# Where a decoder kernel's weight sums leave the DMA queue: five blocks in three early stages, or forty single transfers beside a later feed-forward

## The chip, the core and the metric

One core of a Trainium2 chip runs the whole program. The metric is the device time of one execution in microseconds (us). A time without a range is the median of several runs. TensorE (PE in the profile, PEld for its weight loads), VectorE (DVE), ScalarE (ACT), GpSimd (POOL) and SyncE (SP) each work through a queue of their own. Sixteen DMA engines serve the transfers that SP and POOL issue.

## The reference, cut to what matters

The program is one inference step of a decoder with two layers, over 1024 prompt tokens and 8 sample tokens that share all weights.

- Layer 0 mixes the tokens with a gated linear recurrence and with attention into 256 memory tokens. Layer 1 mixes them with stick-breaking attention over a shared K/V and again with attention into memory.
- After each mixer comes a feed-forward block:

```python
def swiglu(h, w_gu, w_down):
    gate, up = jnp.split(h @ w_gu, 2, axis=-1)
    return (jax.nn.silu(gate) * up) @ w_down
```

The inner width is 2816, so `w_gu` is 1024 x 5632 and `w_down` is 2816 x 1024, for each layer, in float32.

## The kernel before

The tokens are split into two halves. Group 0 is 512 prompt tokens; group 1 is the other 512 and the 8 sample tokens, 520 columns in all. Every product is made of three products in a float32 form with fewer bits: each operand is split into a high part (an ACT cast, line 262 for weights) and a rest (a DVE subtraction, line 263). The weights arrive by `split_w` (line 257, on SP's queue) in tiles of 256 KB, with five raw buffers (`wraw`) and five split buffers (`wspl`).

The feed-forward (`class ffn`) runs in five parts (`PARTS`, of 5, 5, 4, 4 and 4 column blocks). A part first makes its blocks (gate, silu, up, product, split), then multiplies them into all eight rows of blocks of the accumulator `R`. As a generator it yields once a block and once every two rows. `weave` takes several such generators with a number each and draws from the one that is furthest behind its number. That order is the order of the program; a planner then orders the instructions of each engine by priority, buffers and expected times.

**The weight sums.** The last feed-forward, layer 1 of group 1 (`ffn_w`), uses a scheme with seven half-size products in place of eight, and it needs four sums of blocks of layer 1's `w_gu` for each part. `weight_sums` makes them in memory by DMAs alone: eight DMAs a part, issued by POOL, four of them plain copies (line 607) and four accumulating (`accum_op`, line 605). With five parts there are 40 DMAs of 1 MB or 1.25 MB: 10 copies out of the weights, 10 copies of one sum into another, and 20 that accumulate. Within a part most depend on the one before: a sum is copied only when it is complete.

Before a part's eight DMAs stands one mark, a POOL copy of one column (line 592). It reads a row of `R` of group 0's layer 0 feed-forward, so that it can't go before that work is there, and `tc.issue_after` keeps the part's DMAs behind it on POOL.

The order of the stages around it:

1. `a1.sample`, `a1.gate` and `f0.part(1)`, with the sums of part 0
2. `a1.merge`, `a1.mem`, `a1.mem_sample` (the sample tokens' attention into cached memory) and `f0.part(2)`, `f0.part(3)`, with the sums of parts 1 and 2
3. `f0.part(4)`, with the sums of parts 3 and 4
4. the output projection of group 1, the shared K/V of group 0, the projections of layer 1's mixer
5. `b0.sb`, `b0.mem` (layer 1's mixer on group 0) beside `f1.part(0)`, `f1.part(1)` (layer 0's feed-forward on group 1)
6. `f1.part(2)`, `f1.part(3)`, `f1.part(4)` alone

In stage 2 the sample attention (`sample_scores`, lines 911 to 919) writes its queries to memory (`qd`), reads them back broadcast to all partitions for each of the eight sample rows (line 917, SP), and multiplies them with the cache on DVE (line 918). Its cache blocks of 512 KB come over SP's queue too (line 947). POOL also issues the indirect gathers of the shared K/V pages (line 959) for the sample attention of layer 1's mixer on group 1, which comes after stage 6.

Of the kernel before, what the change touches and what calls it, by code (L numbers as in the profile page):

```python
# [1 line left out]

# [15 lines left out]
P = 128  # L18
# [4 lines left out]
def tile_decoder(  # L23
# [6 lines left out]
    nc = tc.nc  # L30
# [39 lines left out]
    def nm(s):  # L70
        uid[0] += 1
        return f"{s}_{uid[0]}"
# [23 lines left out]
    def M(dt=F32):  # L96
        return mpool.tile([P, 2, WID], dt, tag="m", name=nm("m"))
# [4 lines left out]
    def R_one():  # L102
        r = rpool.tile([P, ND, WID], F32, tag="r", name=nm("r"))
        return [r[:, k, :] for k in range(ND)]
# [14 lines left out]
    def small(shape, dt=F32, tag="sm", bufs=None):  # L119
        return spool.tile(shape, dt, tag=tag, name=nm(tag), bufs=bufs)  # L120
# [39 lines left out]
    for lv in range(7):  # L160
        m = 1 << lv
# [17 lines left out]
    def gcol(l, i, k):  # L179
        o = (l * 4 + i) * ND + k  # L180
        return par[:, o : o + 1]
# [43 lines left out]
    def drain(*gens):  # L225
        for g_ in gens:
            for _ in g_:
                pass

    def chain(*gens):  # L230
        for g_ in gens:
            yield from g_

    def weave(*streams):

        live = [[0, n, g_] for g_, n in streams]
        while live:
            cur = min(live, key=lambda e: e[0] / e[1])
            cur[0] += 1
            try:  # L240
                next(cur[2])
            except StopIteration:
                live.remove(cur)


    def pv(ps, g):
        return ps[:, 0, :G] if g == 0 else ps[:, :, : PW[1]]

    def sv(ap, g):
        return ap[:, :G] if g == 0 else ap.rearrange("p (a n) -> p a n", a=2)  # L250
# [17 lines left out]
    def proj(g, W, k0, nk, m0, xt):  # L268
        w = split_w(W, k0, nk, m0)
        ps = mmp.tile([P, 2, 512], F32, tag="mm", name=nm("mm"))  # L270
        for k in range(nk):
            wh, wl = w[k]
            for wi, (wt, xi) in enumerate(((wh, 0), (wh, 1), (wl, 0))):
                for a in range(NPC[g]):
                    o = a * PW[g]
                    nc.tensor.matmul(  # L276
                        ps[:, a, : PW[g]], wt, xt[k][:, xi, o : o + PW[g]],
                        start=(k == 0 and wi == 0), stop=(k == nk - 1 and wi == 2),
                    )
        return ps  # L280

    def split_to(dst, src):
        nc.scalar.copy(dst[0], src)  # L283
        nc.vector.tensor_sub(dst[1], src, dst[0].bitcast(F32))  # L284

    def silu(dst, ps, g):


        n = NG[g]
        x = T()  # L290
        dst = T() if dst is None else dst
        d = dst[:, :n]
        nc.vector.tensor_scalar(sv(x, g), pv(ps, g), -44.0, None, op0=ALU.max)  # L293
        nc.scalar.activation(d, x[:, :n], AF.Exp, scale=-1.0)
        nc.scalar.activation(d, d, AF.Ln, bias=1.0)
        nc.scalar.activation(d, d, AF.Exp, scale=-1.0)  # L296
        nc.vector.tensor_mul(d, d, x[:, :n])  # L297
        return dst
# [11 lines left out]
    def sq_acc(acc, src, k, n):  # L310
        if k == 0:
            nc.scalar.activation(acc[:, :n], src, AF.Square)
        else:
            t = N()
            nc.scalar.activation(t[:, :n], src, AF.Square)  # L315
            nc.vector.tensor_add(acc[:, :n], acc[:, :n], t[:, :n])  # L316
# [125 lines left out]
    def evac_raw(g, R, ps, m, acc, first, last):  # L442
        n = NG[g]
        dst = sv(R[m], g)
        if first:
            nc.scalar.copy(dst, pv(ps, g))
        else:
            nc.vector.tensor_add(dst, dst, pv(ps, g))  # L448
        if last:
            sq_acc(acc, R[m][:, :n], m, n)  # L450
# [74 lines left out]
    def gate_up_w(l, f, ops, spl, raws):  # L525

        h, n = PW[1], NG[1]
        part, o = part_of(f)
        gate, up = f * P, DFF + f * P
        src = [  # L530
# [58 lines left out]
    def weight_sums(l, parts, after):  # L589

        for i in parts:
            mark = nc.gpsimd.tensor_copy(small([P, 1], tag="mk", bufs=1), after()[:, 0:1])
            f0, nf = PARTS[i]
            w = nf * P
            s1, s2, s3, s4 = (tc.dram_tile([512, w], F32, name=nm("wsum")) for _ in range(4))
            sums.setdefault(l, {})[i] = (s1, s2, s3, s4)
            a11, a12 = (w_gu[l][r : r + 512, f0 * P : f0 * P + w] for r in (0, 512))
            a21, a22 = (w_gu[l][r : r + 512, DFF + f0 * P : DFF + f0 * P + w] for r in (0, 512))
            for d, a, add in (
                (s3, a11, False), (s1, a21, False), (s3, a21, True), (s1, a22, True),  # L600
                (s2, s3, False), (s2, a22, True), (s4, s2, False), (s4, a12, True),
            ):
                with tc.issue_after(mark.ins):
                    if add:
                        nc.gpsimd.dma_start(d, a, accum_op=ALU.add)
                    else:
                        nc.gpsimd.dma_start(d, a)
                yield

    htok = []  # L610
# [76 lines left out]
    class ffn:  # L687
# [4 lines left out]
        def part(self, pi):  # L692
            g, l = self.g, self.l
            n = NG[g]
            f0, nf = PARTS[pi]
            last = pi == len(PARTS) - 1
            mids = []
            for j in range(nf):
                pg = proj(g, w_gu[l], 0, ND, (f0 + j) * P, self.xt)
                sg = silu(None, pg, g)  # L700
                pu = proj(g, w_gu[l], 0, ND, DFF + (f0 + j) * P, self.xt)
                nc.vector.tensor_mul(sv(sg, g), sv(sg, g), pv(pu, g))  # L702
                mt = M(F32R)
                split_to((mt[:, 0, :n], mt[:, 1, :n]), sg[:, :n])
                mids.append(mt)
                yield
            if pi == 0:
                self.R = R_one()
            if last:
                self.acc = small([P, WID], tag="st", bufs=3)  # L710
            for m in range(ND):
                ps = proj(g, w_down[l], f0, nf, m * P, mids)
                evac_raw(g, self.R, ps, m, self.acc, pi == 0, last)
                if last and self.rows:
                    nc.scalar.activation(
                        self.R[m][:, :n], self.R[m][:, :n], AF.Copy, scale=gcol(l, 3, m)
                    )
                    if m == 3:
                        first_half(self)
                if m % 2:  # L720
                    yield
# [9 lines left out]
    def first_half(self):  # L731
        self.yt = [xpool.tile([P, D], F32, tag="x0", name=nm("yT")) for _ in range(CH)]
        for c in range(CH):
            ps = S()
            for k in range(4):
                nc.tensor.transpose(ps[:, k * P : (k + 1) * P], self.R[k][:, c * P : (c + 1) * P], ident)  # L736
            nc.scalar.copy(self.yt[c][:, :512], ps)
        self.ys = xpool.tile([P, D], F32, tag="x0", name=nm("yTs"))
        ps = S()
        for k in range(4):  # L740
            nc.tensor.transpose(ps[:NB, k * P : (k + 1) * P], self.R[k][:, G : G + NB], ident)
        nc.scalar.copy(self.ys[:NB, :512], ps[:NB, :])
# [647 lines left out]
    a1 = mixer_a(1, x1)  # L1390
# [5 lines left out]
    f0 = ffn(0, 0, o0.x)  # L1396
    weave((a1.core(), 22), (f0.part(0), 9))
    a1.open()
    def running():
        return f0.R[0]  # L1400

    weave((a1.sample(), 6), (a1.gate(), 4), (f0.part(1), 9), (weight_sums(1, (0,), running), 8))
    weave(
        (chain(a1.merge(), a1.mem()), 12), (a1.mem_sample(), 20), (chain(f0.part(2), f0.part(3)), 16),
        (weight_sums(1, (1, 2), running), 16),
    )
    weave((f0.part(4), 8), (weight_sums(1, (3,4), running), 16))
    xk0, xb0 = [], []
    o1 = out_proj(1, 0, M)
    drain(o1.mm(a1.xo, 0, 1))  # L1410
# [4 lines left out]
    b0 = mixer_b(0, xb0)  # L1415
    weave((b0.heads(), 8), (o1.finish(), 17))
    b0.open()
    f1 = ffn(1, 0, o1.x)
    weave((chain(b0.sb(), b0.mem()), 24), (chain(f1.part(0), f1.part(1)), 18))
    drain(f1.part(2), f1.part(3), f1.part(4))  # L1420
    xk1, xb1 = [], []
    o0 = out_proj(0, 1, M)
    drain(o0.mm(b0.xo, 0, 1))
# [7 lines left out]
    f0 = ffn(0, 1, o0.x)  # L1431
# [9 lines left out]
    f1 = ffn_w(1, o1.x, 4)  # L1441
# [34 lines left out]
```

## Time and profile before

| | |
|---|---|
| median of 3 runs | 2572.91 us (2565.16 to 2581.46) |
| profiled execution | 2567.6 us, span 2565.9 us |
| PE busy | 2513.8 us, 98% |
| PEld, DVE, ACT, POOL busy | 85%, 62%, 47%, 3% |
| DMA | 358.19 MB, mean 140 GB/s |
| queue of SP (hardware_dynamic) | 301.08 MB, 39.6% of the 16 engines' span |
| queue of POOL (software_dynamic) | 54.53 MB, 8.6% |
| mean granted TensorE clock | 0.991 |

How to read it: PE is busy nearly all the time, so a microsecond is to be had only where PE idles or where its granted clock is below one. A view by windows gives, for each stretch of time, the busy time of each engine, the granted clock and the share of time in which the DMA engines moved packets. "A <- B" in a view of waits says that A waited for B.

### The profile page before, as it was taken

The page shows a single profiled execution, that of the slowest core. Times are in us where ns is not written, and L with a number is a line of the kernel's source. Part 1 is how long each engine was busy: PE and PEld are TensorE (multiplying, and loading weights), DVE is VectorE, ACT ScalarE, POOL GpSimd, SP SyncE. Part 2 cuts the span into 40 slices and gives each one's busy share as a digit, 9 for nine tenths or more (in the row PEclk, how much of TensorE's full clock was granted, in tenths as well). Part 3 has the DMA queues.
Part 4 walks back from the last instruction along what each step waited for, and adds up shares of the span by engine and source line. Part 5 has one row for each costly group of instructions (what it writes and reads, how often), then busy time and mean ns, then how long its engine had stood idle before and what let it go on. Part 6 is the DMA issues. An engine that isn't in the chain of part 4 may idle for free. (4 is left out here: it accounts for less than half of the span.)

```text
span 2565.9 us, 40498 instructions
## 1 busy us (share of the span) xinstructions
PE 2513.8 (98%) x15437; PEld 2175.1 (85%) x15437; DVE 1593.6 (62%) x2860; ACT 1215.0 (47%) x2302; POOL 79.2 (3%) x104
## 2 busy tenths in 40 slices
PE   8999999999889999999999999999999999999998
PEld 6888898878666898899999989876676797999998
DVE  6666566654556575656554475777578647845665
ACT  6346543243333454555443354554455445554445
POOL 1000000000010100000000000012000000000000
PEclk9999999999999999999999999999999999999999
DMA  6352242665985996422233436534344334364542
GB/s 185 108 161 71 74 148 76 171 169 165 275 225 156 254 238 193 124 79 78 68 107 91 124 122 190 157 121 141 112 134 127 99 98 137 107 191 143 150 143 71
DMA packets 499884, 358.19 MB, mean 140 GB/s; under 512 B 19077, under 2 KB 451794, under 8 KB 499466
## 3 DMA queue, kind: packets, MB, share of 16 engines
q1 hardware_dynamic: 483466, 301.08, 39.6%
q0 software_dynamic: 16224, 54.53, 8.6%
q8 instruction: 121, 1.98, 0.3%
q14 instruction: 73, 0.60, 0.1%
HBM read 325.73 MB, written 75.94 MB: 157 GB/s over the span
## 5 line engine op out<-in xcount | busy, mean ns | idle before, releaser
L276 PE MATMUL mm<-x,ws 128*128 128x260 f32 (+1 forms) x7968 | 1430.7, 335 | 7.4 <-DVE r L448 3.6
L276 PEld LDWEIGHTS mm<-x,ws 128*128 128x128 f32 x7968 | 1194.1, 189 | 183.6 <-issue 32.3
L262 ACT CAST ws<-w 128x512 fp32r<-128x512 f32 x728 | 429.9, 592 | 726.3 <-PE mm L276 583.2
L263 DVE TENSOR_TENSOR ws<-w,ws 128x512 fp32r<-128x512 f32 x728 | 474.7, 655 | 312.5 <-ACT ws L262 303.1
L276 PE MATMUL mm<-m,ws 128*128 128x512 f32 (+1 forms) x2112 | 419.0, 349 | 8.6 <-DVE r L448 8.6
L276 PEld LDWEIGHTS mm<-m,ws 128*128 128x128 f32 x2112 | 329.6, 190 | 63.2 <-DVE r L448 9.2
L666 PE MATMUL q<-m,ws 128*128 128x260 f32 x1056 | 128.8, 283 | 0.0
L666 PEld LDWEIGHTS q<-m,ws 128*128 128x128 f32 x1056 | 127.2, 188 | 0.4 <-ACT hT L486 0.2
L544 DVE TENSOR_TENSOR ws<-w,ws 128x512 fp32r<-128x512 f32 x126 | 86.5, 692 | 60.2 <-ACT ws L543 54.9
L553 PE MATMUL q<-y,ws 128*128 128x260 f32 x864 | 112.9, 283 | 0.0
L543 ACT CAST ws<-w 128x512 fp32r<-128x512 f32 x126 | 77.9, 621 | 68.1 <-PE q L666 27.0
L553 PEld LDWEIGHTS q<-y,ws 128*128 128x128 f32 x864 | 107.6, 188 | 0.0
L448 DVE TENSOR_TENSOR r<-r,mm 128x512 f32<-128x512 f32 (+1 forms) x96 | 66.1, 689 | 64.9 <-PE mm L276 63.9
L293 DVE TENSOR_SCALAR t<-mm 128x512 f32<-128x512 f32 (+1 forms) x82 | 56.8, 693 | 68.7 <-PE mm L276 68.3
L702 DVE TENSOR_TENSOR t<-t,mm 128x512 f32<-128x512 f32 (+1 forms) x66 | 45.6, 690 | 84.8 <-PE mm L276 84.8
L553 PE MATMUL q<-x,ws 128*128 128x260 f32 x648 | 86.3, 282 | 0.0
L297 DVE TENSOR_TENSOR t<-t,t 128x512 f32<-128x512 f32 (+1 forms) x66 | 45.8, 694 | 60.4 <-ACT t L296 60.4
L553 PEld LDWEIGHTS q<-x,ws 128*128 128x128 f32 x648 | 81.3, 188 | 0.0
L316 DVE TENSOR_TENSOR st<-st,n 128x512 f32<-128x512 f32 (+1 forms) x98 | 67.2, 693 | 6.7 <-ACT n L315 5.0
L283 ACT CAST m<-t 128x512 fp32r<-128x512 f32 (+1 forms) x88 | 54.8, 623 | 22.5 <-DVE t L702 13.6
L284 DVE TENSOR_TENSOR m<-t,m 128x512 fp32r<-128x512 f32 (+1 forms) x88 | 61.1, 695 | 3.0 <-ACT m L283 1.4
L1130 PEld LDWEIGHTS s<-a,a 128*128 128x128 f32 x448 | 53.4, 192 | 1.2
(335 smaller groups left out, 2498.0 us busy)
## 6 DMA issues: line engine op xcount, KB each, us to landing
w<-in_w_gu SPq DMA_DIRECT2D x334, 256.0 KB, 3.0
w<-in_w_down SPq DMA_DIRECT2D x160, 256.0 KB, 2.8
w<-in_w_in_a SPq DMA_DIRECT2D x80, 256.0 KB, 3.0
wsum<-in_w_gu POOLq DMA_DIRECT2D x18, 1024.0 KB, 10.5
w<-wsum SPq DMA_DIRECT2D x72, 256.0 KB, 3.2
w<-in_w_o SPq DMA_DIRECT2D x64, 256.0 KB, 2.8
wsum<-in_w_gu POOLq DMA_DIRECT2D x12, 1280.0 KB, 11.7
w<-in_w_mem_kv SPq DMA_DIRECT2D x32, 256.0 KB, 2.7
```

The lines of the kernel that those rows point to most:

```text
L262: nc.scalar.copy(ws[:, 0, :n, :], raw[:, :n, :])
L263: nc.vector.tensor_sub(ws[:, 1, :n, :], raw[:, :n, :], ws[:, 0, :n, :].bitcast(F32))
L276: nc.tensor.matmul(ps[:, a, : PW[g]], wt, xt[k][:, xi, o : o + PW[g]], start=(k == 0 and wi == 0), stop=(k == nk - 1 and wi == 2),)
L283: nc.scalar.copy(dst[0], src)
L284: nc.vector.tensor_sub(dst[1], src, dst[0].bitcast(F32))
L293: nc.vector.tensor_scalar(sv(x, g), pv(ps, g), -44.0, None, op0=ALU.max)
L316: nc.vector.tensor_add(acc[:, :n], acc[:, :n], t[:, :n])
L448: nc.vector.tensor_add(dst, dst, pv(ps, g))
L543: nc.scalar.copy(w[:, 0, :], src)
L544: nc.vector.tensor_sub(w[:, 1, :], src, w[:, 0, :].bitcast(F32))
L553: nc.tensor.matmul(ps[:, :h], w[:, wj, k * P : (k + 1) * P], x[:, xi, :], start=(first and k == 0 and wi == 0), stop=(k == 3 and wi == 2), ...
L666: nc.tensor.matmul(pp[a][:, :h], wt, mids[k][:, xi, a * h : (a + 1) * h], start=(k == 0 and wi == 0), stop=(k == nf - 1 and wi == 2),)
```

## The change

The early stages lose the sums. They now go out in stages 5 and 6, beside group 1's layer 0 feed-forward: 16 steps of the generator in the first weave, 24 in the second. Each of the 40 DMAs has a mark of its own, and each mark has a step ahead of it: ACT copies one column of what the feed-forward made last (`self.now`, a block's product or a row of `R`) into a small tile `tok` (tag `rr`, three buffers), and POOL's mark copies `tok`. The plain copies get a limit on the length of one descriptor, `4 * w` bytes, which is one row of the part (2560 or 2048 bytes); without it the contiguous copies of one sum into another may go in pieces of up to 64 KB.

```diff
     def weight_sums(l, parts, after):
         for i in parts:
-            mark = nc.gpsimd.tensor_copy(small([P, 1], tag="mk", bufs=1), after()[:, 0:1])
...
             for d, a, add in (
                 (s3, a11, False), (s1, a21, False), (s3, a21, True), (s1, a22, True),
                 (s2, s3, False), (s2, a22, True), (s4, s2, False), (s4, a12, True),
             ):
+                tok = small([P, 1], tag="rr")
+                nc.scalar.copy(tok, after())
+                mark = nc.gpsimd.tensor_copy(small([P, 1], tag="mk", bufs=1), tok)
                 with tc.issue_after(mark.ins):
                     if add:
                         nc.gpsimd.dma_start(d, a, accum_op=ALU.add)
                     else:
-                        nc.gpsimd.dma_start(d, a)
+                        nc.gpsimd.dma_start(d, a, max_dma_last_dim=4 * w)
                 yield
...
                 mids.append(mt)
+                self.now = sg[:, 0:1]
                 yield
...
                 evac_raw(g, self.R, ps, m, self.acc, pi == 0, last)
+                self.now = self.R[m][:, 0:1]
...
-    def running():
-        return f0.R[0]
-
-    weave((a1.sample(), 6), (a1.gate(), 4), (f0.part(1), 9), (weight_sums(1, (0,), running), 8))
-    weave(
-        (chain(a1.merge(), a1.mem()), 12), (a1.mem_sample(), 20), (chain(f0.part(2), f0.part(3)), 16),
-        (weight_sums(1, (1, 2), running), 16),
-    )
-    weave((f0.part(4), 8), (weight_sums(1, (3,4), running), 16))
+    weave((a1.sample(), 6), (a1.gate(), 4), (f0.part(1), 9))
+    weave((chain(a1.merge(), a1.mem()), 12), (a1.mem_sample(), 20), (chain(f0.part(2), f0.part(3)), 16))
+    drain(f0.part(4))
...
     f1 = ffn(1, 0, o1.x)
-    weave((chain(b0.sb(), b0.mem()), 24), (chain(f1.part(0), f1.part(1)), 18))
-    drain(f1.part(2), f1.part(3), f1.part(4))
+    ws = weight_sums(1, range(5), lambda: f1.now)
+    weave((chain(b0.sb(), b0.mem()), 24), (chain(f1.part(0), f1.part(1)), 18), (islice(ws, 16), 17))
+    weave((chain(f1.part(2), f1.part(3), f1.part(4)), 24), (ws, 24))
```

More of the change, by code (lines that the diff above doesn't have):

```diff
@@ L1 @@
 from contextlib import ExitStack
+from itertools import islice
 import concourse.bass as bass
```

## The prediction

> **What bounds the kernel now.** I read the page first, then the kernel by windows. The first line is each engine's busy time; then come the busy tenths of PE and of the DMA engines in forty slices.
>
> ```profile
> PE 2513.8 (98%) x15437; PEld 2175.1 (85%) x15437; DVE 1593.6 (62%) x2860; ACT 1215.0 (47%) x2302; POOL 79.2 (3%) x104
> ...
> PE   8999999999889999999999999999999999999998
> ...
> DMA  6352242665985996422233436534344334364542
> ```
>
> PE is the bound: 52 us of 2565.9 are idle. Slices 11 and 12 (about 640 to 770 us) have an 8, and there the DMA row is high. POOL's timeline (start, length, instruction, idle before it) says when sums are under way; the first and the last issue of each later part:
>
> ```profile
> 623.38 1.29 POOL L607 DMA_DIRECT2D wsum<-in_w_gu  x2
> ...
> 674.09 1.00 POOL L605 DMA_DIRECT2D wsum<-in_w_gu  x1 [6.55 <-DMA wsum<-wsum]
> ...
> 715.41 1.29 POOL L607 DMA_DIRECT2D wsum<-in_w_gu  x2
> ...
> 760.78 1.00 POOL L605 DMA_DIRECT2D wsum<-in_w_gu  x1 [5.61 <-DMA wsum<-wsum]
> ```
>
> With some 10 us for the last to land, a window for each of the five parts (length; busy PE, PEld, DVE, ACT, POOL; clock; DMA share; GB/s):
>
> ```profile
> 475.00:540.00 65.00, 64.99 (x397) 53.18 (x396) 35.39 (x87) 24.07 (x45) 6.91 (x9) 1.00 0.96 239
> 622.00:684.00 62.00, 53.46 (x241) 43.18 (x241) 31.51 (x56) 19.50 (x38) 6.96 (x9) 0.93 1.03 256
> 715.00:770.00 55.00, 47.87 (x197) 35.87 (x196) 29.88 (x50) 15.72 (x34) 6.85 (x9) 0.91 0.98 246
> 818.00:875.00 57.00, 57.00 (x249) 44.32 (x248) 29.66 (x52) 22.22 (x45) 11.40 (x13) 1.00 0.98 248
> 893.00:952.00 59.00, 58.97 (x411) 54.46 (x410) 44.16 (x68) 31.47 (x54) 6.28 (x8) 1.00 1.03 267
> ```
>
> All five fill the DMA engines, but only the second and the third cost PE anything. These lie in the weave with the sample attention. Its waits there, from the views of ACT's, DVE's and PE's timelines, end on transfers:
>
> ```profile
> 655.68 0.62 ACT L262 CAST ws<-w 128x512 fp32r<-128x512 f32 x1 [6.18 <-DMA w<-in_w_gu]
> ...
> 739.32 1.23 DVE L918 TENSOR_TENSOR c<-c,b 128x1024 f32<-128x1024 f32 x1 [11.64 <-DMA b<-qd]
> 740.46 0.68 DVE L448 TENSOR_TENSOR r<-r,mm 128x512 f32<-128x512 f32 x1
> ...
> 741.20 5.06 PE L276 MATMUL mm<-m,ws 128*128 128x512 f32 x11 [7.01 <-DVE r L448]
> ```
>
> A broadcast of queries (`b<-qd`) is late, DVE stands 11.64 us in front of it, the accumulator addition behind it on DVE is late, and PE waits 7.01 us for its PSUM buffer. At 655.68 the weights themselves are late.
>
> **What goes.** Idle PE in the two windows: (62 − 53.46) + (55 − 47.87) = 15.7 us. Below-full clock: 0.07 × 62 + 0.09 × 55 = 9.3 us. Five-microsecond windows show where the clock falls:
>
> ```profile
> 655.00:660.00 5.00, 1.44 (x5) 1.16 (x4) 3.44 (x6) 3.09 (x5) 1.02 (x1) 0.76 1.12 223
> 660.00:665.00 5.00, 5.00 (x14) 3.89 (x14) 1.52 (x3) 0.00 (x0) 0.00 (x0) 0.55 1.11 214
> ...
> 735.00:740.00 5.00, 0.00 (x0) 0.00 (x0) 0.68 (x1) 0.00 (x0) 0.02 (x1) 0.62 1.35 386
> 740.00:745.00 5.00, 3.80 (x9) 3.03 (x10) 5.00 (x6) 0.96 (x4) 0.89 (x1) 0.50 0.51 171
> ```
>
> It falls right behind the gaps and is back within 10 us, so the clock's 9.3 us go where the gaps go: together 25.0 us. The Trainium skill (TensorE: Matmul & The Clock Gate, Part 1: The HAM clock gate) says that the clock halves after an idle window of about 3.4 us and recovers after a busy one as long; 0.55 and 0.50 behind idle times of 3.56 and 7.01 us agree (5.00 − 1.44 and the row above). By that rule a gap cut below the window saves its clock loss whole, and a short new one beside `f1` costs only itself.
>
> What is late next: the sample attention still loads its own blocks. Layer 1 has the same weave, with sample attention twice as long and no sums beside it; and the wait for broadcasts there:
>
> ```profile
> 1650.00:2065.00 415.00, 407.03 (x1639) 289.73 (x1638) 293.75 (x491) 209.08 (x405) 28.02 (x24) 0.99 0.41 121
> ...
> DVE c L918 <- DMA b<-qd: 8.6, 7, 3.8
> ```
>
> It loses 8.0 us idle and 0.01 × 415 = 4.2 us of clock, 2.9%, with a longest broadcast wait of 3.8 us. For 117 us of windows that is 3.4 us. **Net gain: 25.0 − 3.4 = 21.6 us.** Bounds: nothing, if the gaps are the sample loads' own, and 31, if all that 622 to 820 us loses goes (19.4 idle, 11.9 clock):
>
> ```profile
> 622.00:820.00 198.00, 178.58 (x755) 137.58 (x754) 117.62 (x188) 69.98 (x136) 16.32 (x21) 0.94 0.82 217
> ```
>
> **What is added, and where it lies.** The new place begins with layer 1's attention, whose first product (line 1286) starts at 1057.7. Its two windows, in the weave and then alone; then SP's queue and how long weights take to land, first beside sums (818 to 870), then in the new place (1300 to 1497):
>
> ```profile
> L1286 PE MATMUL s<-a,a x96: 271/554/697, 1057.7 to 1984.0; 128*128 128x512 f32 x48, 128*128 128x128 f32 x16, 128*128 128x256 f32 x16, 128*128 128x384 f32 x16
> ...
> 1060.00:1270.00 210.00, 209.01 (x1530) 193.58 (x1529) 120.65 (x242) 111.53 (x228) 0.00 (x0) 1.00 0.25 73
> ...
> 1300.00:1497.00 197.00, 197.00 (x1629) 196.17 (x1629) 98.20 (x144) 75.91 (x121) 0.00 (x0) 1.00 0.35 104
> ...
> q1 hardware_dynamic: 8208, 4.98, 33.9%
> ...
> w<-in_w_gu SPq DMA_DIRECT2D x14, 256.0 KB, 8.3
> ...
> q1 hardware_dynamic: 36981, 20.21, 34.7%
> ...
> w<-in_w_gu SPq DMA_DIRECT2D x34, 256.0 KB, 2.9
> ```
>
> *Contention.* PE has no idle time there, so it can only lose. SP's own load is 34.7% alone and 25% in the weave, against 33.9% in 818 to 870, where PE lost nothing beside sums although weights took 8.3 us instead of 2.9. How late may weights be? A 256 KB tile feeds 24 of `f1`'s products (4 blocks, 3 products, 2 column halves); at 197 / 1629 = 0.121 us each that is 2.9 us, and five raw buffers give some 14.5 us of lead. For group 0 a tile feeds 12 products, by 818 to 875 of 57 / 249 = 0.23 us each, which gives 13.7 us of lead; and 622 to 680, which stalled, had weights landing after
>
> ```profile
> w<-in_w_gu SPq DMA_DIRECT2D x12, 256.0 KB, 13.1
> ```
>
> That is at the lead's end, and 8.3 us is well inside it. Bounds: nothing by 818 to 875; by the windows that stalled 12.5 us for each of five parts, 62 us. I take 1 us, by the row with the same SP share.
>
> *ACT.* Forty copies of one column. Nearest rows: a small ACT instruction, and the mark on POOL:
>
> ```profile
> L754 ACT ACTIVATE rr<-rr x1: 205/205/205, 2556.1 to 2556.1; 128x4 f32<-128x4 f32 x1
> ...
> L592 POOL COPY mk<-r 128x1 f32<-128x1 f32 x5 | 3.1, 616 | 674.6 <-ACT r L446 463.5 <-DVE r L448 211.1
> ```
>
> 40 × 0.2 = 8 us of ACT, which is busy 112 of 210 and 76 of 197 us: hidden by its idle time; without that cover, 8 us. Where `tok` copies a row of `R`, ACT waits for DVE's addition, 0.7 us behind PE, with casts and silu steps queued behind it. The split buffers hold five tiles of lead, so I cost it at nothing.
>
> *POOL.* Thirty-five more marks, 35 × 0.62 = 22 us on a queue that does nothing else then. Behind each mark on POOL stand its DMA and all later ones; a copy also waits for the complete sum before it. The steps of the second weave come after blocks (two tiles each of gate and up, 11.6 us) and pairs of rows (5.8 us), so a part has 4 × 11.6 + 4 × 5.8 = 70 us, where a part's chain, with the last landing after some 10 us, takes 674.09 + 10 − 623.38 = 61 us now. It fits; the sums end some 10 us after `f1`, near 1510. The readers come long after. The page gathers on POOL queue behind them, but the attention that reads them comes with the window of 1650: nothing.
>
> *Short rows.* The ten copies of sums change their pieces. The landing times of line 605 (accumulations) and of line 607 (copies), and the queues' shares during a copy of a sum (497 to 508) and during an accumulation (488 to 497):
>
> ```profile
> DMA to landing us min/median/max: 9.7/11.9/16.8
> ...
> DMA to landing us min/median/max: 5.7/8.9/11.6
> ...
> q0 software_dynamic: 491, 2.40, 79.6%
> q1 hardware_dynamic: 1614, 0.80, 27.9%
> ...
> q0 software_dynamic: 613, 1.52, 91.8%
> q1 hardware_dynamic: 749, 0.36, 17.7%
> ```
>
> Copies land sooner and leave SP more (27.9% against 17.7%), so they are not what crowds it out. I give short rows nothing, between −1 and +1 us. The Trainium skill (DMA: Bandwidth & Descriptors, Queues, rings and completion order) has each DMA engine switch between queues only after a whole packet, so long pieces would hold weights up, and short rows would lower the chance of rival 2 (below) by a few hundredths; these windows put the crowding on the accumulations instead, and I keep it at 8%. The same page (Why small descriptors are slow) puts about 3 cycles on each packet, an estimate of 4% on 2560-byte rows: some 0.4 us a copy, where nobody waits.
>
> **The sum.** 2567.6 − 21.6 + 1 = 2547.0 us for an execution like the profiled one, −0.8%. That execution stood 5.3 us under the median, so against 2572.91 the forecast is **2552 us**. About 1% (25.7 us) is what this measurement tells from no change.
>
> **Rivals.**
>
> 1. *The gaps stay* (22%). DVE waits for its own broadcasts whatever the sums do: SP's queue is in order and the cache blocks are 512 KB. For it: 3.8 us before a PE instruction at 783.52, after the sums had landed.
>
> ```profile
> 783.52 0.30 PE L884 MATMUL s<-ident,b 128*128 128x128 f32 x1 [3.75 <-DVE b L877]
> ```
>
> Against it: layer 1's 3.8 us as the longest wait, 11.6 here. Half the gaps staying gives 2572.9 − 11 + 1 = 2563.
>
> 2. *The contention moves* (8%), the rival on the other side. Weights of `f1` land later than its 14.5 us of lead, as at 655 us, in each of five parts: 2572.9 − 21.6 + 62 = 2613, with two parts of five 2576. It decides when the median landing beside a sum passes some 13 us. For it: PE's slack there is nil and the second weave runs sums nearly all the time. Against it: 8.3 us in the like window. The Trainium skill (DMA: Bandwidth & Descriptors, Issuing engines are not separate DMA queues) says that all queues share the same sixteen engines; the five windows agree on the sharing, and three of them that PE need not pay.
>
> 3. *ACT waits for POOL* (7%). `tok` has three buffers, so ACT's copy waits for the mark three back, which on POOL waits behind DMAs that wait for landings. It decides when POOL lags by three steps, 3 × 5.8 = 17 us, in a run of row pairs. The worst landings are about 12 us for a copy and 17 for an accumulation; a copy, an accumulation and a copy in a row give 40 us, but the mark needed is past the first of them. With one 5 us stall in each part: 2572.9 − 21.6 + 25 = 2576.
>
> 4. *It doesn't go out as said* (3%): the planner puts marks early or late, the transfers bunch, and other queues are ordered anew. About 2568.
>
> **How the numbers follow.** The forecast has 60%, with a range of its own from 2542 (31 us gone, 1 added) to 2562. The range to 2576 takes in rival 1, 4 and the milder 2 and 3; its lower end is 2537, for the spread of the medians. So 2537 to 2576. Faster by over 1% (under 2547.2) is the better third of the forecast and a little more: 34%. Slower by over 1% (over 2598.6) is the hard half of rivals 2 and 3 and an unplanned reordering: 10%. Within 1%: 56%.
>
> **What would show it.** Right: PE busy within 1% of the stretch that replaces 622 to 820, clock 0.98 or better, `b<-qd` waits under 4 us; PE full and clock 1.00 beside `f1`, with DMA share near 0.9 and weights landing in 6 to 10 us; ACT copies without long waits on POOL. Wrong: gaps of 3 us or more in the weave with the sample attention though no sum runs (rival 1); PE waiting for ACT's cast behind a DMA beside `f1` (2); `tok` in ACT's waits with POOL as releaser (3); marks that stand far from their blocks (4).

## The result, and the profile after

The median falls from 2573.52 us to **2538.65 us** (2537.32 to 2539.65). The ratio is 0.9865, with a 95% interval of 0.9833 to 0.9896. The profiled execution takes 2539.07 us, its span is 2537.4 us. The forecast of 2552 us had the direction right and was 13 us short of the gain; the measured time is in the range of 2537 to 2576 us, 2 us above its lower end. The prediction gave a gain of over 1% a chance of 34%; the gain is 1.35%.

The page of the changed kernel, rows as before (its line numbers are one to five higher):

```profile
PE 2503.8 (99%) x15437; PEld 2168.8 (85%) x15437; DVE 1594.9 (63%) x2860; ACT 1220.6 (48%) x2342; POOL 95.6 (4%) x139
...
PE   8999999999999999999999999999999999999998
...
DMA  6352242234644446576678876544343333364542
```

Both 8s in the middle of PE's row are gone. The busy DMA slices have moved from the left half to slices 17 to 24. Span less busy time was 52 us and is 34 us, so 18.5 us of the 28.5 us between the two spans are idle time; the other 10 are shorter busy time of the same 15437 products, which goes with the clock (0.991 before, 0.996 after).

By windows (columns as before): the weave with the sample attention, the weave of `f1` with layer 1's attention, `f1` alone, and layer 1's own sample attention:

```profile
600.00:820.00 220.00, 220.00 (x1001) 170.65 (x1000) 142.26 (x232) 87.66 (x173) 4.10 (x4) 1.00 0.48 141
...
1028.00:1260.00 232.00, 229.84 (x1684) 213.21 (x1683) 130.93 (x262) 121.85 (x265) 22.53 (x34) 1.00 0.67 169
...
1271.00:1487.00 216.00, 216.00 (x1716) 211.43 (x1715) 112.88 (x167) 89.95 (x165) 31.19 (x48) 1.00 0.86 219
...
1625.00:2035.00 410.00, 403.03 (x1627) 286.65 (x1626) 292.00 (x489) 208.31 (x403) 28.21 (x24) 1.00 0.41 122
```

Between 600 and 820 us nothing at all is lost: no idle time, full clock. Beside `f1` alone the DMA engines are at 0.86, and PE has no idle time there either.

The gain between the two profiles lies in one stretch. The last product of the recurrence's sample tokens (line 1081, now 1086) and the first product of layer 1's attention (line 1286, now 1291) start at these times, the first two rows before, the last two after:

```profile
L1081 PE MATMUL s<-c,qd x64: 272/273/421, 535.4 to 613.1; 128*8 128x128 f32 x64
L1286 PE MATMUL s<-a,a x96: 271/554/697, 1057.7 to 1984.0; 128*128 128x512 f32 x48, 128*128 128x128 f32 x16, 128*128 128x256 f32 x16, 128*128 128x384 f32 x16
...
L1086 PE MATMUL s<-c,qd x64: 272/273/421, 535.5 to 613.2; 128*8 128x128 f32 x64
L1291 PE MATMUL s<-a,a x96: 270/556/697, 1028.9 to 1953.8; 128*128 128x512 f32 x48, 128*128 128x128 f32 x16, 128*128 128x256 f32 x16, 128*128 128x384 f32 x16
```

From the one to the other it was 444.6 us and is 415.7 us, which is 28.9 us less; up to the first mark and behind the second nothing is gained on balance.

POOL's timeline at the end of the last part, and one of the two groups of the new ACT step (line 604), with what it waited for and who waited for it:

```profile
1449.88 0.66 POOL L610 DMA_DIRECT2D wsum<-wsum  x1
1455.18 0.57 POOL L605 COPY mk<-rr 128x1 f32<-128x1 f32 x1 [4.63 <-ACT rr L604]
1459.67 1.01 POOL L608 DMA_DIRECT2D wsum<-in_w_gu  x1 [3.92 <-DMA wsum<-wsum]
1460.93 0.56 POOL L605 COPY mk<-rr 128x1 f32<-128x1 f32 x1 [0.24 <-ACT rr L604]
1469.87 0.66 POOL L610 DMA_DIRECT2D wsum<-wsum  x1 [8.38 <-DMA wsum<-in_w_gu]
...
1476.65 1.01 POOL L608 DMA_DIRECT2D wsum<-in_w_gu  x1 [5.93 <-DMA wsum<-wsum]
```

```profile
L604 ACT COPY rr<-r x18: 173/191/203, 1110.7 to 1466.4; 128x1 f32<-128x1 f32 x18
...
  DVE r L449: 0.3, 2
...
  POOL mk L605: 521.0, 36
```

Beside the pairs of rows a transfer waits some 3 to 9 us for the one before it and goes out up to 9 us behind its mark; in the parts before, the next part's blocks, 11 us apart, then let POOL catch up. The ACT step takes 0.19 us, waits 0.3 us in total, and is waited for by POOL alone. The last transfer goes out at 1476.65.

### The profile page after: what moved, and what is told of

Same layout as the page of the kernel before. It is cut to its first block, busy times and chain, and to the rows that moved or that the text cites. A ratio compares the mean times of both kernels' runs of the same rounds, so it can differ in the third digit from the quotient of the medians.

```text
span 2537.4 us, 40627 instructions
## 1 busy us (share of the span) xinstructions
PE 2503.8 (99%) x15437; PEld 2168.8 (85%) x15437; DVE 1594.9 (63%) x2860; ACT 1220.6 (48%) x2342; POOL 95.6 (4%) x139
## 3 DMA queue, kind: packets, MB, share of 16 engines
q0 software_dynamic: 18560, 54.53, 9.0%
## 5 line engine op out<-in xcount | busy, mean ns | idle before, releaser
L277 PEld LDWEIGHTS mm<-x,ws 128*128 128x128 f32 x7968 | 1190.5, 188 | 175.0 <-issue 28.5
L964 POOL DMA_INDIRECT c<-in_cache_sb_k,pidx x16 | 16.4, 1025 | 1015.4 <-DVE x L285 796.7
```

The source lines that it names most:

```text
L277: nc.tensor.matmul(ps[:, a, : PW[g]], wt, xt[k][:, xi, o : o + PW[g]], start=(k == 0 and wi == 0), stop=(k == nk - 1 and wi == 2),)
```

## The experiments

Two theories stood against each other. **Place**: accumulations that meet another stage's transfers hold PE up, and beside `f1` there is little to meet. **Form**: single marks and short rows make the transfers mild wherever they run. A third, **load**, says that sums cost PE in proportion wherever they run. The ratios are with the kernel before on the same chip; the medians of before on the chips used lie between 2570.5 and 2573.5 us.

**1. Place without form.** One mark a part, no ACT step, no limit on the pieces, at the new place.

```diff
         for i in parts:
+            mark = nc.gpsimd.tensor_copy(small([P, 1], tag="mk", bufs=1), after())
...
-                tok = small([P, 1], tag="rr")
-                nc.scalar.copy(tok, after())
-                mark = nc.gpsimd.tensor_copy(small([P, 1], tag="mk", bufs=1), tok)
...
-                        nc.gpsimd.dma_start(d, a, max_dma_last_dim=4 * w)
+                        nc.gpsimd.dma_start(d, a)
```

> The sums stand beside group 1's layer 0 feed-forward as in the change, but in the old form: one mark a part, read straight from the feed-forward, no ACT step, no limit on the pieces. Place theory (the loss was the meeting of two parts of sums with layer 0's sample attention, nothing else): 2536 to 2543 us, as the change, PE without idle time in the stretch of the sample attention and less than 4 us idle beside the feed-forward. Form theory (single marks and short rows are what spares PE): 2549 us or more, with PE waiting for weights beside the feed-forward while a part's eight transfers run in a block.

Measured: 2543.01 us (2540.57 to 2544.66), ratio 0.9885 (0.9847 to 0.9923): at the place theory's bound of 2543, and 6 us under the form theory's. The same kernel and the change on one chip:

> The old form (a mark a part, no ACT step, no limit on the pieces) at the new place once more. If the form is worth something of its own: 2 to 6 us over the change on the same chip, intervals apart. If not: within 2 us of it.

> The change itself, on the same chip as the next one. 2537 to 2541 us.

Measured: 2542.28 us (2540.95 to 2545.92) against 2538.67 us (2537.02 to 2541.53) for the change; ratios 0.9883 (0.9864 to 0.9903) and 0.9871 (0.9852 to 0.989). The medians are 3.6 us apart; the ranges overlap by half a microsecond and the intervals of the ratios overlap, so the times alone do not settle the size. The profiles show a place for it. The window of the weave with layer 1's attention in the two profiles of the old form at the new place, and from the second of them two waits and the longest gap:

```profile
1028.00:1260.00 232.00, 228.46 (x1665) 211.61 (x1664) 129.38 (x258) 119.48 (x245) 13.80 (x18) 1.00 0.66 168
...
1028.00:1260.00 232.00, 226.23 (x1656) 209.81 (x1655) 128.46 (x257) 118.90 (x244) 13.84 (x18) 1.00 0.65 166
```

```profile
ACT ws L263 <- DMA w<-in_w_gu: 5.3, 2, 2.9
...
PE s L1304 <- ACT b L284: 5.1, 3, 3.1
```

```profile
1076.49 0.62 ACT L263 CAST ws<-w 128x512 fp32r<-128x512 f32 x1 [2.91 <-DMA w<-in_w_gu]
...
1078.74 0.50 PE L1304 MATMUL s<-b,trir 128*128 128x512 f32 x1 [3.11 <-ACT b L284]
```

3.5 and 5.8 us are idle here, against 2.2 and 1.0 in the two profiles of the change. While a part's eight transfers run in a block the weights are late; in the longest gap ACT stands 2.91 us before a weight tile, and the step of the attention that follows it is late for PE. So place is nearly the whole gain (29 of 33 us), and form is worth up to 4 us.

**2. Which element of the form.** The change with one element undone.

```diff
-                tok = small([P, 1], tag="rr")
-                nc.scalar.copy(tok, after())
-                mark = nc.gpsimd.tensor_copy(small([P, 1], tag="mk", bufs=1), tok)
+                mark = nc.gpsimd.tensor_copy(small([P, 1], tag="mk", bufs=1), after())
```

> The change without the ACT step: each mark on POOL reads the feed-forward's tile itself. Place theory: nothing, 2536 to 2542 us. If the small tile matters because a mark on POOL that stands behind a transfer holds the feed-forward's buffer meanwhile: PE waits for buffers beside the feed-forward, 2545 us or more.

Measured: 2538.21 us, ratio 0.9871 (0.9855 to 0.9888).

```diff
-                        nc.gpsimd.dma_start(d, a, max_dma_last_dim=4 * w)
+                        nc.gpsimd.dma_start(d, a)
```

> The change without the limit on the pieces of the plain copies. By the prediction (short rows are worth nothing, between -1 and +1 us): 2537 to 2541 us. If long pieces hold up the transfers of the stick-breaking attention and of the weights: PE idle beside the feed-forward 3 us or more (1.8 in the change), 2542 us or more, as in the run with the old form at the new place.

Measured: 2538.87 us, ratio 0.9879 (0.9863 to 0.9896). The limit does change the pieces: POOL's queue moves the same 54.53 MB in 18560 packets with it and in 16224 without. Neither the ACT step nor the short rows is worth anything that can be measured beside the change's 2538.67. By elimination, what is left of the form is that the marks are single; undoing both at once was not tried.

**3. Form without place.** The three early stages keep the sums, with a mark and an ACT step for each, drawn one by one from one generator.

```diff
-    weave((a1.sample(), 6), (a1.gate(), 4), (f0.part(1), 9))
+    ws = weight_sums(1, range(5), lambda: f0.now)
+    weave((a1.sample(), 6), (a1.gate(), 4), (f0.part(1), 9), (islice(ws, 8), 8))
...
+        (islice(ws, 16), 16),
...
-    drain(f0.part(4))
+    weave((f0.part(4), 8), (ws, 16))
```

> The sums stay in the three early stages, in the new form: a mark and an ACT step for each transfer, short rows, one step of the generator at a time. Place theory: the accumulations meet the sample attention as before, 2558 to 2575 us, with 8 us or more of idle PE between 622 and 820 us. Form theory: most of the gain is there, 2540 to 2552 us.

Measured: 2565.75 us (2561.88 to 2569.02), ratio 0.9973 (0.9958 to 0.9988). The median is 6 us less than before. Its windows, two lines of its waits between 880 and 960 us, and the two gaps there with the late ACT instruction ahead of each:

```profile
600.00:820.00 220.00, 211.85 (x940) 162.84 (x939) 135.98 (x219) 83.99 (x180) 23.47 (x37) 0.98 0.88 235
880.00:960.00 80.00, 68.37 (x438) 61.11 (x437) 51.43 (x81) 35.54 (x67) 12.32 (x19) 0.94 0.94 248
```

```profile
POOL wsum L608 <- DMA wsum<-wsum: 21.4, 3, 8.4
...
ACT rr L604 <- POOL mk L605: 16.1, 4, 8.0
```

```profile
892.55 0.19 ACT L604 COPY rr<-r 128x1 f32<-128x1 f32 x1 [8.00 <-POOL mk L605]
895.33 4.37 PE L277 MATMUL mm<-m,ws 128*128 128x512 f32 x12 [5.08 <-DVE r L449]
...
935.71 0.62 ACT L263 CAST ws<-w 128x512 fp32r<-128x512 f32 x1 [4.87 <-DMA w<-in_w_o]
939.32 2.08 PE L306 MATMUL ns<-st,ones 128*128 128x512 f32 x2 [6.55 <-DVE st L317]
```

Idle time between 600 and 820 more than halves (8.2 us), but 11.6 us appear later. At the first gap rival 3 of the prediction happens: ACT's copy waits 8.00 us for POOL (16.1 us in four waits), while POOL itself stands before transfers that have not landed (21.4 us behind copies of sums alone). At the second a late weight tile holds ACT up. From the sample tokens' last product to layer 1's attention this profile needs 444.4 us, as many as before (444.6): single marks at the old place only move the loss. What the 6 us of the medians come from is not shown; the stall of part 0 found in experiment 4 is absent here, where its first sum goes out at 549 us and not at 476.

**4. Part by part.** Only parts 1 and 2 move, in the new form; then parts 0, 1 and 2. The others stay as before (`weight_sums_old` is the old function).

```diff
+    weave((a1.sample(), 6), (a1.gate(), 4), (f0.part(1), 9), (weight_sums_old(1, (0,), running), 8))
...
+    weave((f0.part(4), 8), (weight_sums_old(1, (3, 4), running), 16))
...
+    ws = weight_sums(1, (1, 2), lambda: f1.now)
+    weave((chain(b0.sb(), b0.mem()), 24), (chain(f1.part(0), f1.part(1)), 18), (ws, 17))
```

> Only the sums of parts 1 and 2 move beside group 1's layer 0 feed-forward, in the new form; parts 0, 3 and 4 stay in the early stages in the old form. Place theory: these two were the only ones that cost PE anything, so 2536 to 2544 us. Load theory (sums cost PE in proportion wherever they run in the early stages): two fifths of the gain, about 2559 us.

Measured: 2550.29 us (four times 2549.7 to 2552.1, once 2542.82), ratio 0.9911 (0.9879 to 0.9942). Neither theory's number, but for one execution: too slow for place as the prediction had it, too fast for load. Its windows:

```profile
450.00:540.00 90.00, 85.23 (x514) 72.88 (x512) 49.03 (x133) 27.73 (x52) 6.90 (x9) 0.96 0.74 180
600.00:820.00 220.00, 220.00 (x1001) 170.66 (x1000) 143.25 (x234) 88.32 (x174) 4.87 (x6) 1.00 0.54 153
880.00:960.00 80.00, 77.21 (x495) 67.95 (x494) 57.57 (x90) 38.01 (x67) 4.10 (x5) 1.00 0.83 214
```

The stretch of the sample attention is clean, but part 0's window has 4.8 us idle at a lower clock, where the first profile of before had none, and the last parts' window 2.8 us. Hence the next two.

> Parts 0, 1 and 2 move beside group 1's layer 0 feed-forward in the new form; parts 3 and 4 stay beside group 0's last part in the old form. With two parts moved the time was 2550 us, and its profile and that of the run with one broadcast show a stall of 4.7 us near 505 us that the profile of before lacks. If part 0's sums stall PE there in most executions: 2539 to 2544 us, no idle time between 450 and 540 us. If the 11 us left with two parts moved are those of parts 3 and 4: 2546 to 2551 us, with the loss between 880 and 960 us.

Measured: 2542.85 us (2539.36 to 2546.06), ratio 0.9884 (0.986 to 0.9908).

> The kernel before, profiled once more. If its stalls are a matter of which transfer meets which: gaps at other places or of other lengths than in the first profile, above all an idle time of 4 to 5 us near 505 us, with a total of idle PE between 15 and 35 us. If they are fixed: the same 19.4 us between 600 and 820 us and none near 505 us.

Measured: 2575.8 us, one execution. Windows of this second profile of the kernel before, and ACT's and PE's timelines around its new gap:

```profile
450.00:540.00 90.00, 84.50 (x509) 72.40 (x508) 48.32 (x132) 27.23 (x51) 6.91 (x9) 0.96 0.72 177
600.00:820.00 220.00, 199.33 (x871) 153.90 (x869) 124.11 (x198) 77.71 (x148) 13.98 (x18) 0.95 0.77 204
```

```profile
508.62 0.62 ACT L262 CAST ws<-w 128x512 fp32r<-128x512 f32 x1 [5.72 <-DMA w<-in_w_in_a]
```

```profile
510.27 0.79 PE L1169 MATMUL s<-a,b 128*128 128x128 f32 x2 [5.49 <-DVE b L1170]
```

A weight tile of `w_in_a` is late, ACT stands 5.72 us before it, the gate's work behind it on ACT and DVE is late, and PE waits 5.49 us. The first profile of before did not have this, and two later profiles of programs with the same start (parts 1 and 2 moved; one broadcast, below) have it again at the same place. So part 0's sums do stall PE, in some executions: in three of the four profiles with them in this place, and in none of the ten without. By the medians, parts 1 and 2 cost 21.3 us (2571.6 to 2550.3), part 0 costs 7.4 (to 2542.9) and parts 3 and 4 cost 4.2 (to 2538.7). These steps are rough: they come from two chips, the last is within the overlap of the ranges, and the first compares medians that hold part 0's stall in different numbers of executions. The table behind experiment 7 has them by profile.

**5. No sums.** The last feed-forward reads plain blocks of the weights; the sums' transfers, marks and ACT steps are left out.

```diff
+    for i, (c0, nf) in enumerate(PARTS):
+        sums.setdefault(1, {})[i] = tuple(
+            w_gu[1][r : r + 512, c + c0 * P : c + (c0 + nf) * P] for r in (0, 512) for c in (0, DFF)
+        )
```

> No sum is made: the last feed-forward reads plain blocks of the weights in the place of the four sums, so the transfers of the sums, their marks and ACT steps are left out and everything else stays. Place theory: beside the feed-forward the sums cost some 1 us of PE, so 2535 to 2539 us. Load theory: the moved sums still cost 5 us or more, 2533 us or less.

Measured: 2535.88 us (2535.48 to 2537.92), ratio 0.9861 (0.9824 to 0.9899). By the medians the forty transfers beside `f1` cost about 3 us at most, with ranges that overlap; the span of 2534.2 us is 3.2 under the first profile of the change and 1.1 under the second (2535.3). Most of the 3.2 us is not the sums': layer 1's attention starts 2.6 us earlier here (1026.3 against 1028.9), and the change issues its first sum only at 1044.70. No better place could bring more than these 3 us.

**6. The bad place once more.** The sums in the new form beside layer 1's sample attention.

```diff
+    ws = weight_sums(1, range(5), lambda: f0.now)
     weave(
         (chain(b1.sb(), b1.mem()), 40), (chain(b1.sb_sample(), b1.mem_sample()), 39),
-        (chain(f0.part(0), f0.part(1), f0.part(2), f0.part(3)), 34),
+        (chain(f0.part(0), f0.part(1), f0.part(2), f0.part(3)), 34), (ws, 40),
     )
```

> The sums in the new form, but beside layer 1's sample attention and group 0's layer 1 feed-forward (40 steps against 39 of the sample attention), where no sums ever ran; the early stages are free of them as in the change. Place theory (accumulations and the sample attention's own transfers collide): the gaps come back there, 2550 to 2575 us, with over 18 us of idle PE in the 410 us of that weave (7 in the change) and waits for the broadcasts of queries above 6 us. Load theory (the early stages were special, any later place is free): 2537 to 2543 us.

Measured: 2611.85 us, ratio 1.0164 (1.0147 to 1.0181): slower than before, 73 us over the change, and far beyond what either theory expected. The window of that weave, and waits between 1625 and 2110 us:

```profile
1625.00:2035.00 410.00, 348.47 (x1321) 247.90 (x1320) 247.18 (x410) 182.59 (x367) 69.87 (x88) 0.92 0.75 197
```

```profile
DVE c L923 <- DMA b<-qd: 48.5, 11, 11.7
POOL c L964 <- ACT rr L604: 44.3, 3, 20.9
...
PE s L1306 <- ACT b L284: 35.8, 7, 11.1
...
DVE c L935 <- DMA c<-in_cache_sb_v,pidx: 20.7, 3, 8.6
```

61.5 us idle where the change has 7.0, at a clock of 0.92. DVE stands 48.5 us before broadcasts. The stick-breaking attention in the same weave is a chain of short steps through DVE, ACT and PE, so PE feels each wait. One more route is new: the page gathers (line 964) share POOL's queue with the marks, 44.3 us of POOL's idle time before gathers ends with an ACT step for a mark, and DVE stands 20.7 us before pages. How the 73 us divide between the two routes stays open.

**7. The broadcasts.** The kernel before, with one broadcast of queries in place of eight in layer 0's sample attention.

```diff
-            qb = B()
-            nc.sync.dma_start(qb, qd[b].partition_broadcast(P))
+            if b == 0 or not one:
+                qb = B()
+                nc.sync.dma_start(qb, qd[b].partition_broadcast(P))
```

> The kernel before, with one of the eight broadcasts of queries in layer 0's sample attention; all eight sample rows there use the first row's queries, so seven transfers of 256 KB are left out. If DVE standing before a late broadcast is what hands the contention on to PE: 5 to 15 us less than before, 2557 to 2567 us, and the 7 us gap near 740 us gone. If late weights and late cache blocks would do the same without it: within 4 us of before, 2568 us or more, with gaps of 3 us or more still there between 622 and 820 us.

Measured: 2559.9 us (2553.57 to 2567.59), ratio 0.9955 (0.9939 to 0.9971): 10.6 us less. Its windows and a wait between 600 and 820 us:

```profile
622.00:684.00 62.00, 56.14 (x263) 45.60 (x261) 29.70 (x54) 20.59 (x40) 6.96 (x9) 0.94 0.98 247
715.00:770.00 55.00, 53.66 (x232) 40.44 (x231) 31.40 (x55) 17.77 (x38) 6.96 (x9) 1.00 0.91 232
```

```profile
ACT ws L262 <- DMA w<-in_w_gu: 15.7, 7, 7.9
```

The second window has 1.3 us idle where it had 7.1, so its gap goes with the broadcasts. The first keeps 5.9 of 8.5: there it is late weights. Both are transfers that are late beside the sums. The run leaves out seven transfers as well as the waits for them, and does not tell the two apart.

**All profiles by three stretches.** Each is a difference of two start times that the profiles give, in us, with lines as in the kernel before. *Part 0*: from the last product of line 1130 to the first of line 1081. *Early*: from the last of line 1081 to the first of line 1286, which holds the early sums but part 0's. *f1*: from there to the last product of gate and up of `f1` (line 702).

| profile | part 0 | early | f1 |
|---|---|---|---|
| before | 41.3 | 444.6 | 411.9 |
| before, second profile | 49.1 | 445.1 | 411.9 |
| single marks at the old place | 41.3 | 444.4 | 411.9 |
| one broadcast | 48.2 | 432.1 | 411.8 |
| parts 1 and 2 moved | 48.4 | 419.5 | 411.9 |
| parts 0 to 2 moved | 41.3 | 420.1 | 411.8 |
| the change, two profiles | 41.3, 41.3 | 415.7, 415.8 | 413.1, 412.0 |
| the change without ACT step; with long rows | 41.3, 41.3 | 415.7, 415.7 | 412.0, 411.9 |
| old form at the new place, two profiles | 41.3, 41.3 | 415.7, 415.7 | 414.7, 416.8 |
| no sums | 41.3 | 415.7 | 411.9 |

So parts 1 and 2 cost 25 us, parts 3 and 4 another 4 once these are gone, and part 0 costs 7 to 8 us in an execution that stalls. With single marks the sums cost 0 to 1.2 us beside `f1`, in the old form 3 to 5.

## Why the prediction was right, and where its size was off

**The mechanism: right.** The gaps in the two windows of the sample attention went with the sums, the clock's loss with the gaps, and beside `f1` the sums are nearly free. The signs that it named are there: no idle time and a clock of 1.00 between 600 and 820 us, 2.1 us of waits for `b<-qd` there, a DMA share of 0.86 beside `f1` alone, and ACT copies that don't wait for POOL. How long weights take to land beside `f1` the views do not give, but nothing waits for them.

**The two windows: too small.** They were to bring 21.6 us. The step of the medians, 21.3, looks like a hit and is in part luck, since the profiles give 25 us for these two parts. I left 3.4 us for the sample attention's own waits, and nothing is left in the stretch of 600 to 820; the bound of 31 us, for all that 622 to 820 us lost, was close for that stretch by itself. In exchange 2.8 us appear between 880 and 960 with two parts moved and 3.3 with three; that the stall ahead had shielded this later stretch is my reading, not shown.

**The three other windows: wrong.** "Only the second and the third cost PE anything" was read from one execution, and I priced parts 0, 3 and 4 at nothing. Parts 3 and 4 cost 4 us once the others are gone, though the profile of before has no idle time in their windows. Part 0 costs 7 to 8 us in executions that stall. The same step made "the sum" carry the 5.3 us between the profiled execution and the median along as a fixed distance. It was no such thing: the profiled execution was one without part 0's stall, and the change's stands 0.4 us from its median. The spread of the runs had it in plain sight, 2565 to 2581 us. Of the 13 us that are missing, about 3.5 are parts 1 and 2, 4 are parts 3 and 4, and 5 are this distance.

**The cost beside `f1`: 1 us, measured 0 to 1.2.** PE is full beside `f1` alone, with DMA engines at 0.86, as the window of 818 to 875 said. What cost there is lies in the weave with layer 1's attention: 2.2 us idle in one profile of the change, against 1.0 without sums and 1.0 in the change's second profile. Short rows at nothing and the ACT step at nothing: both right, within a microsecond of the medians.

**Rivals.** Rival 1 (the gaps stay) fell: with no sums near, even the gap that I cited for it is gone. Rival 2 (the contention moves) was true of another place: beside layer 1's sample attention the sums cost 73 us more than beside `f1`. Rival 4 (another order than said) shows no sign: the marks go out from 1044 to 1471 us, beside `f1`. Rival 3 (ACT waits for POOL) does not happen in the change and does happen with the same marks at the old place.

The Trainium skill (TensorE: Matmul & The Clock Gate, Part 1: The HAM clock gate) lets the clock fall after an idle window of some 3.4 us. Two windows agree: one gap of 5.49 us took that of 450 to 540 to 0.96, while 5.8 us in pieces of at most 3.1 us left 1.00. One more does not, and is told in the last section.

The Trainium skill's other rule that was weighed (DMA: Bandwidth & Descriptors, Queues, rings and completion order) is that a DMA engine switches between queues only after a whole packet. That long pieces would therefore hold other queues up is not borne out by the run with long rows (2538.87 us against 2538.67).

## What to carry to other kernels

In this kernel background transfers cost next to nothing beside a feed-forward whose weights arrive with buffers ahead. Beside chains that read back what they have just written, or that wait on transfers in the order of a queue, the same bytes cost tens of microseconds. Price a contended stretch by several executions, not by the one that was profiled: a wide spread of the times before was here the sign of stalls that come and go. When a stall is removed, look for a new one in the stretches behind it.

## What the runs showed of the hardware that was not expected

The same instructions at the same place either stall or don't. The kernel before, with part 0's sums beside the gate, has no idle PE between 450 and 540 us in one profile and 5.5 us in the next, with a late weight tile as the cause. The times fit: the kernel before spread over 20 us (2565.32 to 2585.13 in 14 runs), the kernel without sums over 2.4 us (four runs), the change over 2.3 and 4.5 us (four and five runs).

The clock also falls where PE shows no idle time. Between 535 and 615 us the sample tokens' products use 8 rows or 8 columns (lines 1078 and 1081 of the kernel before), and in eight of the fourteen profiles the clock dips in that stretch, at differing places. The same five microseconds in the first profile of the change and in that without sums:

```profile
560.00:565.00 5.00, 5.00 (x20) 2.27 (x19) 2.32 (x4) 0.52 (x1) 0.00 (x0) 0.72 0.66 191
...
560.00:565.00 5.00, 5.00 (x28) 3.30 (x28) 2.15 (x5) 0.00 (x0) 0.00 (x0) 1.00 0.87 255
```

A profile with one dip needs 77.7 us from the first to the last product of line 1081, one without needs 76.1 or 76.2, and the one with two needs 79.2. So a dip costs 1.5 us, and it is luck whether an execution has one. That the small products cause it is not shown.
